# A decoder layer on one core: four instead of six plain tiles in the first feed-forward, scalings on ScalarE, and a split held behind a copy

## The chip, the cores and the metric

The kernel runs on one core of one Trainium2 chip. Its time is the device time in microseconds (us); for the kernel before it is the median of three runs. A profile is one execution, taken by the hardware profiler. The engines are PE (TensorE, matrix multiplication, with PEld for its weight loads), DVE (VectorE), ACT (ScalarE), POOL (GpSimd) and SP, which only issues DMAs.

## What is computed

The reference is one layer of a decoder on 512 tokens of width 1024, all in float32. Cut to what matters here:

```python
x = x + 0.5 * swiglu(rms_norm(x, norm_ffn1_w), ffn1_w_in, ffn1_w_out)   # d_ff = 2816
x = x + hybrid_mixer(rms_norm(x, norm_mix_w), ...)                      # Mamba-2 heads and differential attention
x = x + memory_cross_attention(rms_norm(x, norm_cross_w), ...)
x = x + 0.5 * swiglu(rms_norm(x, norm_ffn2_w), ffn2_w_in, ffn2_w_out)
return rms_norm(x, norm_final_w)

def swiglu(h, w_in, w_out):
    gate, up = split(h @ w_in, 2)
    return (silu(gate) * up) @ w_out
```

## The kernel before

**Products.** A float32 value is split into a rounded high part, which ACT copies out, and the remainder, which DVE subtracts; a product is three matmuls (high by high, high by low, low by high), in `mm3` (L312) and `add_product` (L229). The split of a weight is in `split_into` (L152): ACT writes `wh` (L155), DVE writes `wl` (L156). Weights come by DMA into the buffers `wr`, of which there are six; `wh` and `wl` have three each, so a split waits until the product that used the oldest buffer is over.

**Two ways to make two tiles of the first feed-forward.** The 22 tiles of 128 hidden units (each a gate and an up tile) are made in pairs. By plain products (`proj`, L318) one pair takes 2 tiles x (gate, up) x 8 blocks of the contraction x 3 matmuls of 512 columns. By `quad` (L257) it takes seven block products of the Strassen kind, each of 24 matmuls of 256 columns, in the order "11", S1, S2, "12", S3, S4, "22". The seven weights are four blocks from memory, some of them summed by an accumulating DMA that POOL issues (`raw_w`, L243) or on DVE (`t2` L294, `t4` L297), so a quad has seven splits. Between the products ACT copies accumulators: `b_ps` from `a_ps` (L284 in the first quad of the second feed-forward, L289 elsewhere), `p5` (L292) and `u2` (L299). S3 adds to the bank that `u2` is copied from, so S3 waits for that copy.

**The sums that a quad multiplies.** For each of four pairs of input blocks `block_sums` (L218) scales two blocks by the norm's gain (`fe`, `fo`, L221 and L222, on DVE), forms four half-width sums (L206 to L211), and splits them into `s31h/l` and `s24h/l`. The first feed-forward uses it in `ffn1` (L517), the second in `upd_2` (L1222), right behind the output projection of the cross-attention.

**The first feed-forward** (`ffn1`, L489) goes through `THIRDS`: 6, 8 and 8 hidden tiles. With `NPLAIN = 6` the first third is all plain: two tiles in `ffn_first`, and four in the loop at L510, between which the block sums of the four input pairs are written: two pairs ahead of the first of the four tiles, one ahead of the second, one ahead of the third. The other two thirds are four quads each (`ffn_quads`, L435). A third ends in `out_blocks` (L1271), the product with `w_out`, also by seven block products. It begins with "11" and S1 on the first two pairs of hidden tiles, then takes the last pair; the sums of that last pair are made by DVE and ACT while the first ones are multiplied (`block_tiles`, L456). `next(out)`, at L443 or L526, has its first two weights fetched and split early.

**What sets the order.** The program text sets the order on SP and POOL. On PE, DVE and ACT a scheduler deals the instructions out at compile time, in the order of the text as far as it finds them ready in its own reckoning; each engine then runs its list strictly in that order. `behind(ins)` (L184) forces what is issued inside it after the named instructions of the same engine. `Order` (L57) merges the dense stream of matrix products with side chains: a chain's `yield t` asks to be continued `t` us of reckoned PE time later, and `od.spawn(gen, t)` starts it `t` us later. `beside` (L563) starts chains at the end of each third's hidden tiles: `lambdas` (L596, a small DMA and a few tiny DVE and POOL instructions), `early`, `prepare`.

**Ahead of the second feed-forward** `turn(1, summed=True)` (L1235) transposes the last four blocks of the residual on PE, copies them on ACT (L1242), and squares each on ACT (L551) for the next norm; `row_from` (L553) makes the norm's row out of it, which is needed when the first quad's results are gated.

Of the kernel before, what the change touches and what calls it, by code (L numbers as in the profile page):

```python
# [13 lines left out]
AF = mybir.ActivationFunctionType  # L14
ALU = mybir.AluOpType
# [7 lines left out]
MEM = 256  # L23
EPS = 1e-6

NPLAIN = 6

THIRDS = ((0, 6), (6, 8), (14, 8))
THIRDS2 = ((0, 6), (6, 8), (14, 8))
# [71 lines left out]
def body(tc, a, dbg=None):  # L101
# [116 lines left out]
    def block_sums(k0, gain, blocks, x):  # L218

        fe, fo = s2("fe"), s2("fo")  # L220
        V.tensor_scalar(fe, x[k0], par[:, gain + k0 : gain + k0 + 1], None, ALU.mult)  # L221
        V.tensor_scalar(fo, x[k0 + 1], par[:, gain + k0 + 1 : gain + k0 + 2], None, ALU.mult)  # L222
        return blocks | sums_of(fe[:, :H], fe[:, H:], fo[:, H:], fo[:, :H])

    def of_halves(even, odd):
# [3 lines left out]
    def add_product(ps, w, xs, which, first, ks=None):  # L229

        wh, wl = w
        n = len(xs)
        for f in range(2):
            out = ps[:, f * H : (f + 1) * H]
            for kp in ks or range(n):
                wc = slice((f * n + kp) * P, (f * n + kp + 1) * P)
                xh, xl = xs[kp][which]
                for j, (a_, b_) in enumerate(((wh, xh), (wh, xl), (wl, xh))):
                    od.t += (H + 32) / 2400
                    newest_mm[:] = [nc.tensor.matmul(out, a_[:, wc], b_, start=first and f == 0 and kp == 0 and j == 0, stop=kp == n - 1 and j == 2, skip_group_check=True).ins]  # L240
                yield
# [9 lines left out]
    def split_w(raw):  # L251
        hi = wp.tile([P, D], R32, tag="wh", name=nm("wh"))
        lo = wp.tile([P, D], R32, tag="wl", name=nm("wl"))
        newest[:] = [split_into(hi, lo, raw)[0].ins]
        return hi, lo

    def quad(xs, src, ready, fresh=False):  # L257

        b12, b11, b22, b21 = src[0], src[1], src[2], src[3]
        m1 = raw_w(b11)
        if ready:
            t, t2, m2, m7, m3 = raw_w(ready[0]), raw_w(ready[1]), raw_w(b21), raw_w(b12, b22), raw_w(b22)
            t4 = m2
        else:
            t, m3, m2, m7 = raw_w(b12, b11), raw_w(b22), raw_w(b21), raw_w(b12, b22)  # L270
            t2 = t4 = t
        a_ps = acc("qa")
        e_ps = acc("qe")
        b_ps = acc("qb")
        w1, w5 = split_w(m1), split_w(t)
        second = list(newest)
        if fresh:

            n = len(xs)
            yield from add_product(a_ps, w1, xs, "11", True, range(n - 1))  # L280
            yield from add_product(e_ps, w5, xs, S1, True, range(n - 1))
            yield from add_product(a_ps, w1, xs, "11", False, range(n - 1, n))
            with behind(second):
                S.activation(b_ps, a_ps, AF.Copy)  # L284
            yield from add_product(e_ps, w5, xs, S1, False, range(n - 1, n))
        else:
            yield from add_product(a_ps, w1, xs, "11", True)
            with behind(second):
                S.activation(b_ps, a_ps, AF.Copy)  # L289
            yield from add_product(e_ps, w5, xs, S1, True)  # L290
        p5 = s2("p5")
        S.activation(p5, e_ps, AF.Copy)  # L292
        if not ready:
            V.tensor_tensor(t2, t, m3, ALU.add)  # L294
        yield from add_product(b_ps, split_w(t2), xs, S2, False)
        if not ready:
            V.tensor_tensor(t4, t2, m2, ALU.add)  # L297
        u2 = s2("u2")
        S.activation(u2, b_ps, AF.Copy)  # L299
        V.tensor_tensor(e_ps, e_ps, u2, ALU.subtract)  # L300
        yield from add_product(a_ps, split_w(m2), xs, "12", False)
        w7 = split_w(m7)
        if ready:
            V.tensor_tensor(t4, t2, m2, ALU.add)
        yield from add_product(b_ps, w7, xs, S3, False)
        c22 = s2("c22")
        V.tensor_tensor(c22, p5, b_ps, ALU.subtract)
        yield from add_product(e_ps, split_w(m3), xs, S4, False)
        yield from add_product(b_ps, split_w(t4), xs, "22", False)
        yield (a_ps, b_ps), (e_ps, c22)  # L310

# [177 lines left out]
    def ffn1(h, wa, at_out, each, done):  # L489
        xs = []  # L490
        wq, plain = iter(a["f1q"]), a["f1i"]
        col4, ncol4 = small("col4", 4, bufs=1), small("ncol4", 4, bufs=1)

        for ti, (_, nf) in enumerate(THIRDS):
            g = []
            nq = nf // 2
            made = block_tiles(g, nq, True)
            out = out_blocks(a[f"f1b{ti}"], None, g, col4, ncol4, each if ti == len(THIRDS) - 1 else None, n=nq, by_dma=ti == len(THIRDS) - 1)
            if ti == 0:
                th, f = s4("th"), 0  # L500
                for ps in ffn_first(h, wa):
                    if ps is None:
                        yield
                    else:
                        gated(*ps, st1.row, th, f)
                        f += 1
                made(th)
                V.tensor_scalar(col4, st1.col, 0.5, None, ALU.mult)
                V.tensor_scalar(ncol4, st1.col, -0.5, None, ALU.mult)
                for n in range(NPLAIN - 2):  # L510
                    for i in ((0, 1), (2,), (3,), ())[n]:
                        blocks = of_halves(h[2 * i], h[2 * i + 1])
                        b11 = tuple(s2("h11" + p_, R32, (P, H)) for p_ in "hl")
                        with behind(start):
                            for to, of in zip(b11, blocks["11"]):
                                S.activation(to, of.bitcast(F32), AF.Copy)
                        xs.append(block_sums(2 * i, C_FFN1, blocks | {"11": b11}, xf))  # L517
                    if n == 3:
                        xf.clear()
                    pg, pu = acc("pg"), acc("pu")  # L520
                    yield from proj(pg, load_w(plain[n][0]), h)
                    yield from proj(pu, load_w(plain[n][1]), h)
                    if n % 2 == 0:
                        th = s4("th")
                    if n == NPLAIN - 3:
                        next(out)  # L526
                    gated(pg, pu, st1.row, th, n % 2)
                    if n % 2:
                        made(th)
                h.clear()  # L530
                nq -= NPLAIN // 2
            yield from ffn_quads(xs, wq, st1, nq, made, BY_BLOCK, prime=out)
            at_out(ti)
            if ti == len(THIRDS) - 1:
                xs.clear()
            yield from out
        done()
        banks = [acc, aux, acc, aux]
        yield from turn(1, banks)
        yield from turn(0, banks)  # L540
# [12 lines left out]
    def row_from(st, apart, rows=1.2):  # L553
        both = small("nboth", 4, bufs=2)
        V.tensor_tensor(both, squares[:, :4], squares[:, 4:], ALU.add)
        yield from st.from_sums(both, apart, rows)
# [4 lines left out]
    st_mix, h = Stat(), []  # L561

    def beside(ti):  # L563
        if ti == 0:
            od.spawn(lambdas())
        elif ti == 1:
            od.spawn(early())
        elif ti == 2:
            od.spawn(prepare())
            od.spawn(memory_in(hm), 1.0)  # L570
# [25 lines left out]
    def lambdas():  # L596
        lamv = cp.tile([P, 4, 64], F32, name="lamv")
        nc.sync.dma_start(lamv, a["lam"].partition_broadcast(P))
        yield 8.0
        lamp = small("lamp", 64, bufs=2)  # L600
        lsum = small("lsum", 2, bufs=1)
        for j in range(2):
            V.tensor_tensor(lamp, lamv[:, 2 * j, :], lamv[:, 2 * j + 1, :], ALU.mult)
            V.reduce_sum(lsum[:, j : j + 1], lamp, axis=AX.X)
        yield 4.0
        lexp = small("lexp", 2, bufs=1)
        G.tensor_tensor(lexp, euler[:, 0:1].to_broadcast([P, 2]), lsum, ALU.pow)
        yield 4.0
        V.tensor_tensor(nlam, lexp[:, 1:2], lexp[:, 0:1], ALU.subtract)
        V.tensor_scalar(nlam, nlam, -LAMBDA_INIT, None, ALU.add)  # L610
        V.tensor_scalar(wsub, par[:, C_SUBLN : C_SUBLN + 1], 1.0 - LAMBDA_INIT, None, ALU.mult)
        V.tensor_scalar(dskh, par[:, C_DSKIP : C_DSKIP + 8], 0.5, None, ALU.mult)
# [842 lines left out]
            yield from out_blocks(a[f"f2b{c}"], wsum[c], g, col4, ncol4, *((norm, store) if at_end else (None, None)), clean=c == 0)  # L1455

    def turn_last():
        yield from turn(1, summed=True)
        od.spawn(row_from(st_2, 8.0), 3.0)

    od.add(turn_last())
    od.add(ffn2())
# [89 lines left out]
```

## Time and profile before

| | us |
|---|---|
| runs | 1316.0, 1315.11, 1314.69 |
| median of the runs | 1315.11 |
| the profiled execution's own time | 1314.59 |
| its span, from the first to the last instruction | 1312.7 |

The page of the profile gives each engine's busy time and its share of the span. The view of groups gives for each line, operation and tile how often it ran and how long one took. The view of waits says who waited for whom, how long in total and how often. The timeline lists instructions with their start and length in us; in brackets stands how long the engine sat idle ahead of an instruction, and whom it waited for. The view of windows gives each engine's busy time in a stretch. In "qb<-s31h,wh" the tile in front is written and those behind are read.

The matrix products of the first third of the first feed-forward run from 5.61 to 72.17 us, its output product to 100.98, and the second third begins there. The second feed-forward begins at 972.71 us.

### The profile page before, as it was taken

The page shows a single profiled execution, that of the slowest core. Times are in us where ns is not written, and L with a number is a line of the kernel's source. Part 1 is how long each engine was busy: PE and PEld are TensorE (multiplying, and loading weights), DVE is VectorE, ACT ScalarE, POOL GpSimd, SP SyncE. Part 2 cuts the span into 40 slices and gives each one's busy share as a digit, 9 for nine tenths or more (in the row PEclk, how much of TensorE's full clock was granted, in tenths as well). Part 3 has the DMA queues.
Part 4 walks back from the last instruction along what each step waited for, and adds up shares of the span by engine and source line. Part 5 has one row for each costly group of instructions (what it writes and reads, how often), then busy time and mean ns, then how long its engine had stood idle before and what let it go on. Part 6 is the DMA issues. An engine that isn't in the chain of part 4 may idle for free.

```text
span 1312.7 us, 20086 instructions
## 1 busy us (share of the span) xinstructions
PE 1288.3 (98%) x7708; PEld 1123.4 (86%) x7708; DVE 968.9 (74%) x1538; ACT 708.2 (54%) x1208; POOL 127.8 (10%) x157
## 2 busy tenths in 40 slices
PE   9999999999999999999999999999999999999996
PEld 7889988998887778777788877888889999989995
DVE  6987887787776676467867686645668878877886
ACT  7544564565754564346645465434375646555564
POOL 0001010001010011201003022020001000000001
PEclk9999999999999999999999999999999999999998
DMA  9366778876984434753466558683239776666762
GB/s 339 88 168 185 212 184 211 222 199 162 324 291 145 137 64 133 261 166 105 95 189 173 167 141 238 196 222 120 69 99 274 209 231 181 185 193 180 201 192 82
DMA packets 70415, 237.38 MB, mean 181 GB/s; under 512 B 8288, under 2 KB 9792, under 8 KB 69968
## 3 DMA queue, kind: packets, MB, share of 16 engines
q1 hardware_dynamic: 54352, 183.20, 41.7%
q0 software_dynamic: 13168, 45.67, 19.7%
q10 hardware_dynamic: 2800, 7.23, 1.7%
q8 instruction: 60, 0.98, 0.3%
q14 instruction: 35, 0.29, 0.1%
HBM read 233.92 MB, written 50.91 MB: 217 GB/s over the span
## 4 chain that ended last, share of the span: by engine, by line
PE 58%; issue 10%; DVE 4%; ACT 2%; DMA 2%; POOL 1%; POOLq 0%; ACTq 0%; DVEq 0%
PE pm L146 10%; PE qb L240 8%; PE qe L240 5%; PE qa L240 5%; PE pxbc L146 4%; PE ob L1298 3%; PE pcq L146 3%; PE pz L146 3%; PE oe L1298 2%; PE oa L1298 2%; PE pcv L146 2%; PE pq L146 2%; PE pv L146 1%; PE pk L146 1%; DMA wr<-in_f1b 1%
## 5 line engine op out<-in xcount | busy, mean ns | idle before, releaser
L155 ACT ACTIVATE wh<-wr 128x1024 fp32r<-128x1024 f32 (+1 forms) x329 | 334.2, 1019 | 359.3 <-issue 70.6
L156 DVE TENSOR_TENSOR wl<-wr,wh 128x1024 fp32r<-128x1024 f32 (+1 forms) x329 | 384.8, 1173 | 145.3 <-ACT wh L155 140.2
L777 ACT ACTIVATE ec<-ec,mn 128x512 f32<-128x512 f32 (+3 forms) x64 | 35.4, 554 | 33.7 <-DVE mn L776 33.7
L146 PE MATMUL pxbc<-hnh,wh 128*128 128x512 f32 x128 | 52.6, 411 | 0.0
L146 PE MATMUL pxbc<-hnh,wl 128*128 128x512 f32 x128 | 50.3, 393 | 0.0
L146 PE MATMUL pxbc<-hnl,wh 128*128 128x512 f32 x128 | 50.2, 392 | 0.0
L240 PE MATMUL qb<-s31h,wh 128*128 128x256 f32 x152 | 43.2, 284 | 3.2 <-ACT u L299 3.2
L240 PE MATMUL qb<-s24h,wh 128*128 128x256 f32 x152 | 43.1, 284 | 1.3 <-ACT qb L284 1.3
L240 PE MATMUL qb<-s24h,wl 128*128 128x256 f32 x152 | 43.1, 284 | 0.5 <-DVE wl L156 0.5
L240 PE MATMUL qe<-s31h,wl 128*128 128x256 f32 x152 | 43.1, 284 | 0.2 <-DVE wl L156 0.2
L240 PE MATMUL qa<-h11h,wh 128*128 128x256 f32 x152 | 43.1, 283 | 0.0
L240 PE MATMUL qa<-h11h,wl 128*128 128x256 f32 x152 | 43.0, 283 | 0.0
L240 PE MATMUL qa<-hmh,wh 128*128 128x256 f32 x152 | 43.0, 283 | 0.0
L240 PE MATMUL qa<-hml,wh 128*128 128x256 f32 x152 | 43.0, 283 | 0.0
L240 PE MATMUL qe<-s24h,wh 128*128 128x256 f32 x152 | 43.0, 283 | 0.0
L240 PE MATMUL qe<-s24l,wh 128*128 128x256 f32 x152 | 43.0, 283 | 0.0
L240 PE MATMUL qe<-s24h,wl 128*128 128x256 f32 x152 | 43.0, 283 | 0.0
L240 PE MATMUL qb<-hmh,wh 128*128 128x256 f32 x152 | 43.0, 283 | 0.0
L240 PE MATMUL qb<-hml,wh 128*128 128x256 f32 x152 | 43.0, 283 | 0.0
L240 PE MATMUL qb<-hmh,wl 128*128 128x256 f32 x152 | 43.0, 283 | 0.0
L240 PE MATMUL qa<-h11l,wh 128*128 128x256 f32 x152 | 43.0, 283 | 0.0
L240 PE MATMUL qa<-hmh,wl 128*128 128x256 f32 x152 | 43.0, 283 | 0.0
(453 smaller groups left out, 4158.3 us busy)
## 6 DMA issues: line engine op xcount, KB each, us to landing
wr<-in_f2q SPq DMA_DIRECT2D x44, 512.0 KB, 4.5
wr<-in_f1q SPq DMA_DIRECT2D x40, 512.0 KB, 4.3
wr<-in_f1b SPq DMA_DIRECT2D x30, 512.0 KB, 4.3
isum<-in_f2q SPq DMA_DIRECT2D x22, 512.0 KB, 6.2
wr<-isum SPq DMA_DIRECT2D x22, 512.0 KB, 4.6
wsum<-in_f2b SPq DMA_DIRECT2D x20, 512.0 KB, 6.7
wr<-wsum SPq DMA_DIRECT2D x20, 512.0 KB, 4.6
wr<-in_f1q POOLq DMA_DIRECT2D x16, 512.0 KB, 6.5
```

The source lines that it names most:

```text
L146: newest_mm[:] = [nc.tensor.matmul(out, w, x, start=start, stop=stop).ins]
L155: S.activation(hi, src, AF.Copy),
L156: V.tensor_tensor(lo, src, hi.bitcast(F32), ALU.subtract),
L240: newest_mm[:] = [nc.tensor.matmul(out, a_[:, wc], b_, start=first and f == 0 and kp == 0 and j == 0, stop=kp == n - 1 and j == 2, skip_gr ...
L777: S.activation(ec[:, :n], ec[:, :n], AF.Exp, bias=mn, scale=-1.0, accum_out=sm[c][:, i : i + 1])
L1298: newest_mm[:] = [nc.tensor.matmul(ps, a_[:, ts], b_[:, ws], start=first and k == 0 and j == 0, stop=k == n - 1 and j == 2, skip_group_che ...
```

## The change

`NPLAIN` goes from 6 to 4, so the first third is two tiles of `ffn_first`, two plain tiles in the loop and one quad in place of the last two plain tiles; all four block sums are written ahead of the second of the two remaining tiles. `next(out)` moves with it, to the last quad. `block_sums` scales on ACT instead of DVE, in both feed-forwards. In every quad the split of `m3`, the sixth weight, is held behind the copy `u2` on ACT. The chain `lambdas` starts 30 us after the hidden tiles of the second third instead of right after those of the first. The squares ahead of the second feed-forward leave `turn` and become a chain of their own, `row_of_last`, which starts 4 us later, does one square every 2 us, each behind the newest weight split on ACT, and then makes the row.

```diff
-NPLAIN = 6
+NPLAIN = 4
...
     def block_sums(k0, gain, blocks, x):
 
         fe, fo = s2("fe"), s2("fo")
-        V.tensor_scalar(fe, x[k0], par[:, gain + k0 : gain + k0 + 1], None, ALU.mult)
-        V.tensor_scalar(fo, x[k0 + 1], par[:, gain + k0 + 1 : gain + k0 + 2], None, ALU.mult)
+        S.activation(fe, x[k0], AF.Copy, scale=par[:, gain + k0 : gain + k0 + 1])
+        S.activation(fo, x[k0 + 1], AF.Copy, scale=par[:, gain + k0 + 1 : gain + k0 + 2])
...
         u2 = s2("u2")
-        S.activation(u2, b_ps, AF.Copy)
+        copy = S.activation(u2, b_ps, AF.Copy)
...
-        yield from add_product(e_ps, split_w(m3), xs, S4, False)
+        with behind([copy.ins]):
+            w3 = split_w(m3)
+        yield from add_product(e_ps, w3, xs, S4, False)
...
                 for n in range(NPLAIN - 2):
-                    for i in ((0, 1), (2,), (3,), ())[n]:
+                    for i in ((0, 1), (2, 3))[n]:
...
-                    if n == 3:
-                        xf.clear()
...
-                    if n == NPLAIN - 3:
-                        next(out)
                     gated(pg, pu, st1.row, th, n % 2)
...
                 h.clear()
+                xf.clear()
...
-        if ti == 0:
-            od.spawn(lambdas())
-        elif ti == 1:
+        if ti == 1:
+            od.spawn(lambdas(), 30.0)
             od.spawn(early())
...
     def turn_last():
-        yield from turn(1, summed=True)
-        od.spawn(row_from(st_2, 8.0), 3.0)
+        yield from turn(1)
+        od.spawn(row_of_last(), 4.0)
+
+    def row_of_last():
+        for k in range(4, KT):
+            with behind(list(newest)):
+                squared(k, x[k])
+            yield 2.0
+        yield from row_from(st_2, 3.0)
```

## The prediction

> **What bounds the kernel now.** I read the shares of the engines first, then what PE waits for, then the timeline at those waits.
>
> ```profile
> PE 1288.3 (98%) x7708; PEld 1123.4 (86%) x7708; DVE 968.9 (74%) x1538; ACT 708.2 (54%) x1208; POOL 127.8 (10%) x157
> ```
>
> PE is busy 98% of the span. A change can shorten the work that PE does, or close one of its gaps. The view of PE's waits lists the gaps:
>
> ```profile
> PE qb L240 <- ACT u L299: 3.2, 2, 1.6
> ...
> PE qb L240 <- ACT qb L284: 1.3, 1, 1.3
> ...
> PE oe L1298 <- DVE s31l L156: 0.7, 1, 0.7
> ...
> PE qb L240 <- DVE wl L156: 0.5, 1, 0.5
> ...
> PE qe L240 <- DVE wl L156: 0.2, 1, 0.2
> ```
>
> Total, times and longest, in us. Two lines are what this change aims at: two waits for the copy `u2` (3.2 in all) and one for the copy `qb` (1.3). The others are small, so everything else that could be gained is PE's own work.
>
> **The change part by part.**
>
> *A quad in place of two plain tiles.* From the chain of work, one gate or up tile by plain products, and one block product of a quad:
>
> ```profile
> 569.35 5.44 PE pk L146 x24
> ...
> 1067.14 2.88 PE qe L240 x24
> ```
>
> 24 matmuls of 512 columns take 5.44 us (227 ns each), 24 of 256 columns 2.88 us (120 ns each, a little over half). The pair leaves with 4 x 5.44 = 21.76 and the quad comes with 7 x 2.88 = 20.16: **-1.60 us**.
>
> [...]
>
> *The split behind the copy.* The timeline of ACT in a quad that goes well, in one that doesn't, and PE in the latter:
>
> ```profile
> 231.44 1.06 ACT L155 ACTIVATE wh<-wr 128x1024 fp32r<-128x1024 f32 x1 [0.90 <-PE qb L240]
> 232.40 0.58 ACT L299 ACTIVATE u<-qb 128x512 f32<-128x512 f32 x1
> ...
> 251.65 1.06 ACT L155 ACTIVATE wh<-wr 128x1024 fp32r<-128x1024 f32 x1 [1.34 <-issue]
> 252.61 0.61 ACT L155 ACTIVATE s31h<-s 128x512 fp32r<-128x512 f32 x1
> 254.54 1.06 ACT L155 ACTIVATE wh<-wr 128x1024 fp32r<-128x1024 f32 x1 [1.31 <-PE qa L240]
> 255.50 0.58 ACT L299 ACTIVATE u<-qb 128x512 f32<-128x512 f32 x1
> ```
>
> ```profile
> 256.13 0.39 PE L240 MATMUL qb<-s31h,wh 128*128 128x256 f32 x1 [1.58 <-ACT u L299]
> ```
>
> S2 is over at about 251.6 in the second quad, and `u2` could be copied then. But two weight splits stand ahead of it in ACT's list: the sixth, at 251.65, and the seventh, which waits until PE has finished "12" (`qa`). The copy runs at 255.50 and PE is 1.58 late. With the sixth split behind the copy, the seventh, which follows the sixth in the text, comes behind it too. The second occurrence is alike, so both waits go: **-3.15** (3.2 by the row, two waits of just under 1.6). The delayed sixth split costs nothing: the copy puts it off by 0.58, it takes ACT 1.06 and DVE some 1.2, and S4, which uses it, starts two products (5.76) after S2's end. Next late is nothing on PE: "12" runs on meanwhile.
>
> *The squares leave the start of the second feed-forward.* ACT and PE there:
>
> ```profile
> 976.96 0.61 ACT L551 ACTIVATE junk<-x 128x512 f32<-128x512 f32 x1
> ...
> 979.41 0.57 ACT L284 ACTIVATE qb<-qa 128x512 f32<-128x512 f32 x1
> ...
> 987.99 0.60 ACT L407 ACTIVATE row<-nrow 128x512 f32<-128x512 f32 x1 [0.91 <-PE nrow L146]
> ```
>
> ```profile
> 977.71 0.28 PE L240 MATMUL qa<-h11h,wl 128*128 128x256 f32 x1
> ...
> 980.03 0.38 PE L240 MATMUL qb<-s24h,wh 128*128 128x256 f32 x1 [1.33 <-ACT qb L284]
> ```
>
> `qa` is complete at 977.99, but ACT does four squares from 976.96 on, until it copies at 979.41. Without them the copy runs at about 978.05 and ends at 978.65, when PE needs it: **-1.33**, or -1.2 if a square still gets in. The row is then made later: 4.0 + 4 x 2.0 + 3.0 + 1.2 = 16.2 us behind the quad's start at 972.7, some 989, so the copy `row` moves from 987.99 to about 990. It is needed when the quad ends, 20.16 after 972.7, at 992.9. The cover is 3 us; if it were gone, the gating would be late and hold PSUM banks. The four squares then stand among weight splits on an ACT that is 54% busy; I cost them at nothing.
>
> *The scalings go to ACT.* Prices from the timeline: two scalings in a row on DVE, and ACT's operation with a scale column on a tile of the same size:
>
> ```profile
> 37.25 0.48 DVE L221 TENSOR_SCALAR fe<-xf,par 128x512 f32<-128x512 f32 x1
> 37.65 0.48 DVE L222 TENSOR_SCALAR fo<-xf,par 128x512 f32<-128x512 f32 x1
> ```
>
> ```profile
> 4.31 0.72 ACT L159 ACTIVATE hmh<-xf,par 128x512 fp32r<-128x512 f32 x1 [1.99 <-DMA xf<-in_xT]
> ```
>
> Eight per feed-forward: DVE is relieved of 8 x 0.40 = 3.2 us, ACT gets 8 x 0.72 = 5.8. In the second feed-forward this lies beside the output projection, and only the last pair is close to PE:
>
> ```profile
> 976.30 0.69 DVE L156 TENSOR_TENSOR s31l<-s,s31h 128x512 fp32r<-128x512 f32 x1
> ```
>
> It ends at 976.99, and S1 wants it 0.12 behind the `qa` row above, at 977.83. Two scalings of 0.72 take the place of two of 0.40 in its chain, 0.64 longer, which the 0.84 of slack covers; one of the two blocks is ready a tile earlier. I cost it at nothing; uncovered it is 0.6.
>
> *The first third.* Here the engine that matters is DVE. The windows from the end of `ffn_first` to the third plain tile, and from there to `out_blocks` (columns: PE, PEld, DVE, ACT, POOL busy; clock; DMA share; GB/s):
>
> ```profile
> 28.15:50.41 22.26, 22.26 (x99) 18.39 (x98) 20.12 (x43) 13.49 (x22) 1.09 (x1) 1.00 0.48 132
> 50.41:72.17 21.76, 21.76 (x97) 18.02 (x96) 18.07 (x32) 9.68 (x15) 1.84 (x2) 1.00 0.32 80
> ```
>
> DVE is busy 20.12 + 18.07 = 38.19 of 22.26 + 21.76 = 44.02. The fourth pair's sums end like this on DVE:
>
> ```profile
> 56.82 0.69 DVE L156 TENSOR_TENSOR s31l<-s,s31h 128x512 fp32r<-128x512 f32 x1
> 57.42 1.22 DVE L156 TENSOR_TENSOR wl<-wr,wh 128x1024 fp32r<-128x1024 f32 x1
> 58.56 0.69 DVE L156 TENSOR_TENSOR s24l<-s,s24h 128x512 fp32r<-128x512 f32 x1
> ```
>
> The change takes from DVE 3.2 of scalings, four plain splits at 1.14 (57.42 to 58.56), three gating operations of 0.6 (taken as long as the `s31l` from 56.82 to 57.42) and, estimated, 1.0 for the six tiny ones of `lambdas`; it adds seven splits (8.0), two weight sums of the same size (2.3) and three accumulator operations at 0.6 (1.8): 38.2 - 3.2 - 4.6 - 1.8 - 1.0 + 12.1 = 39.7 in 42.4 us. It fits by 2.7. If DVE idles as much as now (44.02 - 38.19 = 5.8), PE is late by 39.7 + 5.8 - 42.4 = **3.1** at most. For the start: the quad begins at 50.41, S1 wants the fourth `s31l` after "11" and nine matmuls, 50.41 + 2.88 + 1.08 = 54.4, S2 the fourth `s24l` at 57.3. Even left where they stand, and only relieved of 3.2, these end at 54.3 and 56.05; the text also puts them one tile earlier. So I take **+0.8** out of 0 to 3.1. ACT goes from 13.49 to at most 19.3 in the first window's 22.26, which fits.
>
> The weights are no wait: the quad's five loads and two accumulating DMAs are asked for behind four loads instead of eight, and land in 9.1 and 6.5 us by these rows, one after the other 15.6, ahead of 50.41 if asked for by 34:
>
> ```profile
> wr<-in_f1q POOLq DMA_DIRECT2D x16, 512.0 KB, 6.5
> ...
> wr<-in_f1i SPq DMA_DIRECT2D x8, 512.0 KB, 9.1
> ```
>
> On SP the two early loads of `out_blocks` now stand behind the quad's five, and are wanted only when the quad ends; `lambdas`' load and POOL's one power move into the second third's output product, between loads issued ahead of need: nothing.
>
> *The end of the first third.* After a quad, gating, the last pair's sums and their splits must be done while PE works on the earlier pairs. Three such ends, PE's first matmul behind the quad and the moment of `s31l`, in the second feed-forward's first third, and the first one's second and third thirds:
>
> ```profile
> 1035.52 0.40 PE L1298 MATMUL oa<-wh,g11h 128*128 128x512 f32 x1
> ...
> 1042.34 0.39 PE L1298 MATMUL oe<-wh,s31h 128*128 128x512 f32 x1
> ```
>
> ```profile
> 1041.41 0.69 DVE L156 TENSOR_TENSOR s31l<-s,s31h 128x512 fp32r<-128x512 f32 x1
> ...
> 193.05 0.69 DVE L156 TENSOR_TENSOR s31l<-s,s31h 128x512 fp32r<-128x512 f32 x1
> ...
> 315.17 0.69 DVE L156 TENSOR_TENSOR s31l<-s,s31h 128x512 fp32r<-128x512 f32 x1
> ```
>
> ```profile
> 183.09 0.40 PE L1298 MATMUL oa<-wh,g11h 128*128 128x512 f32 x1
> ...
> 307.02 0.40 PE L1298 MATMUL oa<-wh,g11h 128*128 128x512 f32 x1
> ```
>
> With three pairs the cover is 1042.34 - 1035.52 = 6.82. `s31l` was done after 6.58, 10.65 and 8.84, the last two with weight sums in between on DVE, as here, though half of ours are half as wide. The cost is 0 to 10.65 - 6.82 = 3.83; between the nearest two (0 and 2.0) I take **+1.0**. A plain end has no such wait.
>
> Sum: -1.60 - 3.15 - 1.33 + 0.8 + 1.0 = **-4.28**. Against the profiled execution's own 1314.59 (span 1312.7) that is 1310.31; the median of the runs stands 0.52 higher, 1315.11, and gives **1310.8 us**.
>
> **The rivals.**
>
> *No new wait at all*: -6.08, or -7.5 if the 0.5, 0.2 and 0.7 in the waits go as well in the new order: 1307.6 to 1309.0. For it: DVE's slack, and the 6.58 against 6.82. Against: 96% of DVE asked for in a strict order.
>
> *The first third pays it back*: DVE late by the full 3.1 and the end by 3.83: -6.08 + 6.93 = +0.85, 1316.0.
>
> *The edge does not free the copy*: the scheduler deals the seventh split, which has no edge of its own, ahead of `u2` again. The seventh was what held it at 254.54. Then 3.15 stays: -1.1, 1314.0. Against: it comes behind the sixth in the text.
>
> *Slower: DVE waits for ACT at each scaling.* The scalings are now at the head of each pair's chain and in ACT's strict list, behind copies and splits that themselves wait. The same handover in DVE's waits:
>
> ```profile
> DVE wl L156 <- ACT wh L155: 140.2, 145, 4.7
> ```
>
> That is 0.97 each. If each of the eight scalings of the first third costs DVE that much, 7.8 come on top of 3.1: -6.08 + 10.9 = +4.8, **1319.9**. It decides from 8.7 of new waits on, which turns the sign past 0.2%. Against: `xf` has long landed, so ACT can scale ahead of need; it is free for 22.26 - 13.49 = 8.8 us of the first window. [...]
>
> **How the numbers follow.** Forecast 0.50; no new wait 0.12; paid back 0.14; edge fails 0.07; slower 0.17. 0.2% is 2.6 us, about what a measurement of this kernel can tell from no change. So faster 0.62, same 0.21, slower 0.17. The range from 1307.5 to 1318 takes in all but the slower rival and a few lucky cases.
>
> **What would show it.** Right: the quad's seven products of 2.88 us from about 50.4; no row of PE waiting for `u` L299, nor for `qb` L284; DVE at 9 tenths or more from 28 to 70 us; a wait of `oe` or `oa` for `g11l` or `s31l` near 77 us of 0 to 2. Wrong: waits of PE for `wl`, `s31l`, `s24l` in the first quad that add up to more than 3, or a later part, whose order this change should leave alone, dealt differently.

## The result, and the profile after

| | kernel before | kernel after |
|---|---|---|
| median of four runs each | 1315.55 us | 1329.3 us |
| lowest and highest | 1314.69, 1317.23 | 1324.54, 1332.88 |
| profiled execution | 1314.59, span 1312.7 | 1332.88, span 1330.8 |

The ratio of the times is 1.0099, with an interval of 1.0076 to 1.0123: the change makes the kernel about 1% slower, where 0.3% faster was forecast. The profiled execution is the longest of the four.

The view of PE's waits of the kernel after (total, times, longest, in us) answers to the five lines shown of before:

```profile
PE qe L240 <- ACT gate L430: 5.3, 1, 5.3
PE ob L1296 <- ACT wh L155: 5.2, 2, 4.2
...
PE ob L1296 <- DVE wl L156: 1.1, 1, 1.1
PE oa L1296 <- ACT g11h L155: 1.0, 1, 1.0
...
PE qb L240 <- ACT qb L284: 0.8, 1, 0.8
PE oa L1296 <- DVE g11l L156: 0.8, 1, 0.8
```

What the change aimed at came about: no row for `u` L299 is left, and the copy `qb` L284 costs 0.8 instead of 1.3. But there are two new waits of over 4 us, and some of about 1.

The view of windows, cut at PE's first matmul of six stages of the first feed-forward, shows where the time went. The stages are the last two tiles of the first third (plain before, a quad now), the first third's output product, the second third's quads and output product, and the third third's. Columns are PE, PEld, DVE, ACT, POOL busy, then the granted clock, DMA share and GB/s. First the kernel after, then the rows of before that the prediction does not show:

```profile
52.77:80.68 27.91, 22.64 (x170) 22.34 (x169) 21.07 (x31) 13.06 (x18) 0.86 (x1) 0.88 0.31 83
80.68:111.11 30.43, 29.33 (x130) 23.69 (x128) 26.70 (x38) 15.73 (x22) 2.57 (x3) 1.00 0.69 186
111.11:193.45 82.34, 81.15 (x674) 80.74 (x673) 68.50 (x82) 45.39 (x56) 7.76 (x9) 1.00 0.73 193
193.45:235.51 42.06, 40.30 (x171) 32.60 (x169) 32.35 (x41) 19.87 (x23) 3.15 (x4) 0.96 0.75 205
235.51:318.17 82.66, 81.63 (x674) 80.97 (x673) 67.81 (x84) 45.90 (x63) 8.00 (x10) 1.00 0.77 197
318.17:366.70 48.53, 43.21 (x174) 33.22 (x173) 36.35 (x50) 27.16 (x45) 4.24 (x5) 0.93 0.82 235
```

```profile
72.17:100.98 28.81, 28.81 (x128) 23.84 (x127) 24.68 (x35) 14.44 (x20) 2.61 (x3) 1.00 0.74 203
...
183.09:222.50 39.41, 38.71 (x170) 31.38 (x169) 33.02 (x39) 20.10 (x23) 3.45 (x4) 1.00 0.81 220
222.50:307.02 84.52, 81.37 (x675) 80.91 (x674) 66.36 (x81) 46.59 (x63) 6.91 (x8) 1.00 0.80 206
307.02:347.75 40.73, 40.21 (x174) 31.36 (x173) 34.92 (x49) 27.24 (x45) 4.30 (x5) 1.00 0.79 234
```

Read pairwise: the quad that took the place of two plain tiles takes 27.91, not less than the pair's 21.76 (+6.15). The first third's output product has 1.6 more, the second third's 2.65. The third third's quads, where the two waits for `u2` were, have 1.86 less. The third third's output product has 7.8 more. Three of the rows of after have a granted clock below 1.00, and the rows of before have none. These five differences add up to 16.4 of the 18.1 by which the spans differ. Another 2.4 stands at the very start of this execution, where PE's matmuls of 512 columns begin 0.43 us apart up to 11.1 us, while in the kernel before they begin 0.23 apart from 7.05 on, and the loop's plain tiles begin at 30.97 instead of 28.61; the later versions of the changed kernel, with the same start, have them between 28.5 and 29.3, so this is no effect of the change. The rest of the kernel is about 0.7 shorter.

**The first quad.** The timeline of the kernel after, PE and then DVE:

```profile
61.31 0.55 PE L240 MATMUL qe<-s31h,wh 128*128 128x256 f32 x1 [5.27 <-ACT gate L430]
...
56.41 1.22 DVE L297 TENSOR_TENSOR wr<-wr,wr 128x1024 f32<-128x1024 f32 x1
...
58.14 1.22 DVE L156 TENSOR_TENSOR wl<-wr,wh 128x1024 fp32r<-128x1024 f32 x1
59.28 0.69 DVE L156 TENSOR_TENSOR gl<-th,gh 128x512 fp32r<-128x512 f32 x1
...
60.48 0.68 DVE L435 TENSOR_TENSOR th<-pu,gate 128x512 f32<-128x512 f32 x1
```

The pool `acc` has four PSUM banks. The plain tiles' `pg` and `pu` have them all, so the quad's `qa` gets the bank of the first `pg`, and `qe`, which S1 writes, that of the first `pu`. That `pu` is read for the last time by the product at L435, 60.48 to 61.16, and S1 starts at 61.31. All that it reads was there some 12 us earlier: `pu` was complete at 42.05, and its gate was begun on DVE at 47.26. But it writes `th`, of which there is one buffer, and that buffer is still read by `gl`, the split of the two tiles before; and `gl` stands behind the last pairs' sums and the quad's own weight sums in DVE's list. The kernel before has the same chain, and nobody waits, since `gl` runs at 50.76 and the product is over at 52.64:

```profile
50.76 0.69 DVE L156 TENSOR_TENSOR gl<-th,gh 128x512 fp32r<-128x512 f32 x1
...
51.96 0.68 DVE L433 TENSOR_TENSOR th<-pu,gate 128x512 f32<-128x512 f32 x1
```

Its next `pu` takes that bank at 55.85, with 3.2 to spare. Now `gl` comes 8.5 later (59.28), and the 3.2 become the 5.3 that PE waits. Counted from the stage's first matmul, `gl` comes 6.2 later (6.51 instead of 0.35), and the bank is wanted 2.2 sooner, since "11" is shorter than the `pg` that stood there. (The view names the ACT gating at L430 as the releaser, that of the second tile. It ended last, at 61.23, but it works on `gate`, which is in no PSUM bank; the run with a second buffer below shows that the chain is the one described.)

**The clock behind it.** The windows of after ahead of S1, during S1, and during S2:

```profile
55.90:61.31 5.41, 0.14 (x1) 0.03 (x1) 5.31 (x8) 2.68 (x5) 0.00 (x0) 0.80 0.14 34
61.31:66.30 4.99, 4.99 (x25) 4.99 (x26) 1.74 (x4) 0.73 (x2) 0.00 (x0) 0.54 0.04 16
66.30:69.20 2.90, 2.90 (x27) 2.90 (x26) 1.66 (x3) 2.06 (x3) 0.00 (x0) 1.00 0.00 0
```

S1 takes 4.99 instead of 2.88 at a granted clock of 0.54. The wait of 5.27 costs 2.1 more than itself.

**The last output product.** The timelines of before and of after around the second of the two weight sums for S2 (the `wr<-wr,wr` on DVE). It frees a `wr` buffer, into which SP loads (L1279, L1277) the second part of the weights for S3; POOL accumulates on it (L1318, L1316); ACT splits it.

```profile
315.77 1.22 DVE L1328 TENSOR_TENSOR wr<-wr,wr 128x1024 f32<-128x1024 f32 x1
...
317.02 0.33 SPq L1279 DMA_DIRECT2D wr<-in_f1b  x1
...
322.37 0.86 POOL L1318 DMA_DIRECT2D wr<-in_f1b  x1 [2.07 <-DMA wr<-in_f1b]
...
331.91 1.06 ACT L155 ACTIVATE wh<-wr 128x1024 fp32r<-128x1024 f32 x1 [2.29 <-DMA wr<-in_f1b]
```

```profile
331.77 1.22 DVE L1326 TENSOR_TENSOR wr<-wr,wr 128x1024 f32<-128x1024 f32 x1
...
333.02 0.33 SPq L1277 DMA_DIRECT2D wr<-in_f1b  x1
...
340.11 0.86 POOL L1316 DMA_DIRECT2D wr<-in_f1b  x1 [7.56 <-DVE hm L160]
...
348.77 1.06 ACT L155 ACTIVATE wh<-wr 128x1024 fp32r<-128x1024 f32 x1 [8.49 <-DMA wr<-in_f1b]
...
349.88 0.79 PE L1296 MATMUL ob<-wh,s31h 128*128 128x512 f32 x1 [4.22 <-ACT wh L155]
```

The output product begins at 307.02 and 318.17. Counted from there, the sum came at 8.75 and comes at 13.6 now; SP's load starts as it ends, 10.0 and 14.85; POOL's accumulation comes at 15.35 and 21.9, and ACT's split at 24.9 and 30.6. PE waits 4.22, and runs the next 6.2 us at a granted clock of 0.50.

### The profile page after: what moved, and what is told of

It is laid out like the page before. It is cut to its first block, busy times and chain, and to the rows that moved or that the text cites. A ratio compares the mean times of both kernels' runs of the same rounds, so it can differ in the third digit from the quotient of the medians.

```text
span 1330.8 us, 20257 instructions
## 1 busy us (share of the span) xinstructions
PE 1295.8 (97%) x7780; PEld 1131.9 (85%) x7780; DVE 972.0 (73%) x1528; ACT 721.6 (54%) x1229; POOL 130.4 (10%) x159
## 4 chain that ended last, share of the span: by engine, by line
PE 72%; issue 14%; DVE 6%; DMA 3%; ACT 3%; POOL 2%; POOLq 0%; SPq 0%; ACTq 0%; DVEq 0%
PE qb L240 12%; PE pm L146 10%; PE qe L240 8%; PE qa L240 8%; PE pxbc L146 4%; PE ob L1296 4%; PE oa L1296 4%; PE pcq L146 3%; PE pz L146 3%; PE oe L1296 3%; DVE wl L156 2%; PE pa L146 2%; PE pcv L146 2%; PE pq L146 2%; DMA wr<-in_f1q 1%
## 5 line engine op out<-in xcount | busy, mean ns | idle before, releaser
L240 PE MATMUL qe<-s31h,wh 128*128 128x256 f32 x160 | 46.3, 290 | 5.3 <-ACT gate L430 5.3
L240 PE MATMUL qe<-s31h,wl 128*128 128x256 f32 x160 | 46.3, 289 | 0.7 <-DVE wl L156 0.7
L240 PE MATMUL qe<-s31l,wh 128*128 128x256 f32 x160 | 46.2, 289 | 0.0
L240 PE MATMUL qb<-s31l,wh 128*128 128x256 f32 x160 | 45.3, 283 | 0.0
L240 PE MATMUL qb<-s31h,wl 128*128 128x256 f32 x160 | 45.3, 283 | 0.0
```

## The experiments

Each kernel is timed against the kernel before on the same chip. The kernel before came to 1315.22, 1316.46 and 1316.64 in three sets of runs made for this, so a difference between medians of different sets is good to about 1 us. My theory after the result was that three things had gone wrong separately: the bank behind `th` in the first quad, DVE's list in the last output product, and the clock behind each. The rivals were that one edit (the four plain tiles, or the scalings) costs the time by its work, or that the split's new place does not gain.

**The split behind the copy alone** (the kernel before with the edit of `quad`)

```diff
-        S.activation(u2, b_ps, AF.Copy)
+        copy = S.activation(u2, b_ps, AF.Copy)
...
+        with behind([copy.ins]):
+            w3 = split_w(m3)
```

> The kernel before with the edge alone: the sixth split behind the copy u2. Theory (the change's parts gain as priced, the loss comes from the first third and what its waits set off): both waits of PE for the copy, 3.15 us, go, so about 3.2 less than the kernel before, 1312.3, and no row of PE waiting for u. Rival (the edge deals the whole ACT list anew and costs elsewhere): no gain, or 1316 and more.

Measured: 1321.7 us (1315.27 to 1324.75), ratio 1.004 [1.0023, 1.0057]. The expectation failed, and its rival (a list dealt anew that costs elsewhere) came true, though in DVE's list. The rows for `u` L299 are gone, but this edit alone brings the late weights of the last output product. Its timeline there, where the output product begins at 305.78:

```profile
320.72 1.22 DVE L1330 TENSOR_TENSOR wr<-wr,wr 128x1024 f32<-128x1024 f32 x1
...
321.96 0.33 SPq L1281 DMA_DIRECT2D wr<-in_f1b  x1
...
329.81 0.86 POOL L1320 DMA_DIRECT2D wr<-in_f1b  x1 [8.05 <-DMA wr<-in_f1b]
...
338.84 1.06 ACT L155 ACTIVATE wh<-wr 128x1024 fp32r<-128x1024 f32 x1 [9.61 <-DMA wr<-in_f1b]
...
339.95 0.80 PE L1300 MATMUL ob<-wh,s31h 128*128 128x512 f32 x1 [5.33 <-ACT wh L155]
```

The edit stands in another function than the weight sum. The scheduler reckons the whole program through, and with the quads reckoned differently it deals the second sum out behind two updates of `x` and some splits, at 14.9 instead of 8.75.

**The squares in a chain alone** (the kernel before with the edits of `turn_last` and `row_of_last`)

> The kernel before with only the four squares moved out of the turn into a chain of their own. Theory: the wait of 1.33 for the copy qb shrinks to the 0.8 that the changed kernel shows, so 0.5 to 1.3 us less, within the noise of one run: 1314.2 to 1315.0. Rival (the row comes too late and the gating of the first quad holds PSUM): PE waits of over 1 us behind 990 us, 1316 to 1318.

Measured: 1314.93 us, ratio 0.9998 [0.9989, 1.0008]; the wait for `qb` L284 is 0.8 instead of 1.3. So the edit gains 0.5 of a wait where I gave it 1.33, too little for the times to show, and does no harm. ACT's timeline in the changed kernel shows what is late next, a weight split that itself waits until PE is done with `qa`:

```profile
996.38 1.06 ACT L155 ACTIVATE wh<-wr 128x1024 fp32r<-128x1024 f32 x1 [0.26 <-PE qa L240]
997.34 0.58 ACT L284 ACTIVATE qb<-qa 128x512 f32<-128x512 f32 x1
```

**Four plain tiles alone** (the kernel before with `NPLAIN = 4` and the loop that goes with it; the scalings on DVE, `lambdas` in the first third)

> The kernel before with four instead of six plain tiles alone (block sums of all four pairs ahead of the second of the two tiles, scalings still on DVE, lambdas, squares and the split as before). Theory (the quad in the first third brings the wait for its bank and what follows it): -1.6 for the products, +5 to +9 for the wait since eight scalings of 0.4 stand in DVE's list again, +2 for the clock, 0 to 3 at the thirds' ends: 1321 to 1328. Rival (the scalings on ACT are the cause): without them the quad fits, 1314 to 1316.

Measured: 1325.88 us, ratio 1.0084 [1.006, 1.0108]. PE's longest wait in it:

```profile
PE qe L240 <- DVE lamp L600: 7.0, 1, 7.0
```

The wait for the bank is there without the other edits, and is longer (7.0 against 5.3), so the other edits taken together shorten it. It isn't all that this kernel loses: the second third's quads, which were not edited, take 86.4 against 82.1, with a wait of 1.88 for a weight's split and a granted clock of 0.54 in the 6.3 us behind it. (The releaser named, `lamp`, is the DVE instruction that came last; it writes no bank.)

**The changed kernel with a buffer of its own for the plain tiles' product**

```diff
                     if n % 2 == 0:
-                        th = s4("th")
+                        th = s4("gate")
```

The buffer of that name is free until the first quad's gating.

> The changed kernel, with the result of the two plain tiles of the loop written to the idle buffer named gate instead of the single buffer th. Theory: the 5.27 us that S1 of the first quad waits are a chain of buffers (S1's bank is free once the plain tile's th is written, th once the last split of the tiles before has read it), and the 2.26 that S1 then takes longer are the clock at half after the idle stretch. With the second buffer both go: 1329.3 - 7.5 = 1321.8, and PE's S1 follows 11 within 1 us. Rival (DVE is simply full, the buffer only the last in line): PE waits as long for s31l or wl of the quad, 1328 and more.

Measured: 1321.79 us, ratio 1.005 [1.0031, 1.0069], 7.5 below the changed kernel. The wait of 5.27 and the half clock behind it are gone (the matmuls of S2 and S1 there begin 0.12 us apart); this shows the chain from `gl` through `th` to the bank: `gl` is as late as ever (57.55), but the product of the first `pu` runs at 46.56. The scheduler now also deals S2 to PE ahead of S1, so next late is S2:

```profile
PE qb L240 <- ACT qb L289: 2.5, 2, 1.8
```

The 1.8 is in the first quad: ACT's copy stands behind the fourth `s24h`, which waits for DVE's last pair of sums. This is the lateness of DVE that the prediction had named.

**The changed kernel with PE kept busy in the wait.** 23 more matmuls of ones go into the bank that `out_blocks` clears, in the first third alone; nothing reads them.

```diff
-        if clean:
+        for _ in range(24 if early and sums[3] is not None and n == 3 and not by_dma else 1 if clean else 0):
             nc.tensor.matmul(b_ps[1], ones_r, ...)
```

> The changed kernel with 23 more matmuls of ones into the cleared bank, dealt to PE where it waits 5.3 us in the first quad. They compute nothing that is used. Theory (the half clock behind that wait comes from PE having been idle): the first quad's S1 starts as late as before but takes 2.9 to 3.1 us instead of 5.14, the granted clock there is 1.0, and the time is 1329.3 less 2.3, about 1327. Rival (the clock is lowered by something else, the load of the stretch ahead): S1 still takes about 5 and the time stays at 1329.

Measured: 1324.95 us (1321.03 to 1327.19, against 1324.54 to 1332.88 of the changed kernel), ratio to before 1.0062 [1.0043, 1.0081]. The windows of the filled wait and of S1 behind it:

```profile
53.96:59.63 5.67, 5.65 (x27) 4.35 (x25) 5.57 (x9) 2.81 (x5) 0.00 (x0) 1.00 0.13 33
59.63:62.60 2.97, 2.97 (x25) 2.97 (x26) 1.74 (x4) 0.74 (x2) 0.00 (x0) 1.00 0.07 26
```

S1 starts as late behind "11" as in the changed kernel and takes 2.97 at a granted clock of 1.00, against 4.99 at 0.54. So here the half clock came with PE's idling, and not from the work around it. The gain of 4.4 is more than the 2.3 expected, but the runs of both kernels spread by 6 to 8; the profile also has a granted clock of 1.00 from 50 to 340 us, the end of the second third in it, where the changed kernel has 0.73 from 199.76 to 206.00.

**Both weight sums ahead of the updates** (the kernel before with the split behind the copy)

```diff
+        by_t2 = sums[2]
+        if here:
+            w2 = {part: t2(part) for part in parts}
+            by_t2 = lambda part: w2[part]
         for t in range(2):
             update(t + 2, 1, e_ps[t], 1, False)
-        yield from product(b_ps, sums[2], S2)
+        yield from product(b_ps, by_t2, S2)
```

> The kernel before with the split behind the copy alone, and in the output product of a third both weight sums for S2 taken ahead of the two updates of x. Theory (the split's new place re-deals DVE's list, so that the second weight sum of the last third falls behind the updates, and the load that needs its buffer goes out 5 us late): the second sum comes about 9 us after the end of the last third's quads instead of 14.9, ScalarE's wait for the last accumulated weights falls from 9.6 to about 2.5, PE's 5.3 at the output's last products is gone and so is the half clock behind it; 1321.7 falls by 5.3 + 3 to about 1313. Rival (the late weights come from the queue of accumulating transfers or from SP's loads, not from the sum's place): the wait of 5.3 stays and the time is within 1 us of 1321.7.

Measured: 1314.54 us, ratio 0.9988 [0.9979, 0.9997], some 7 below the run with the split alone. PE's wait of 5.33 and the half clock behind it are gone; the mean granted clock of the profiled execution is 0.997, against 0.995 with the split alone. The second sum comes at 11.2 (the output product begins at 303.79), earlier than 14.9 but not as early as the 9 that I expected. PE now waits for something smaller, the first part's split, which DVE does behind both sums and the updates:

```profile
315.03 1.22 DVE L1330 TENSOR_TENSOR wr<-wr,wr 128x1024 f32<-128x1024 f32 x1
...
319.76 0.50 PE L1300 MATMUL ob<-wl,s24h 128*128 128x512 f32 x1 [2.10 <-DVE wl L156]
```

Nothing but the place of the sums and their loads in the text was changed, so it is that place that made the 5.3. The last output product takes 51.22 in the run with the split alone, 43.31 here and 40.73 in the kernel before, so in this stage the new place takes back most of what the split had cost and gains nothing beyond it. The new place without the split was not run.

**The same with the squares in a chain**

> As the one before, with the squares of the second turn in a chain of their own as well. Theory: the gains add, 3.15 at the copies of the sixth product, less about 0.9 of new waits for the seventh, and 0.5 at the squares: 2 to 3 below the kernel before, 1312 to 1313. Rival (a wait removed in this list comes back somewhere else each time): 1315 to 1322.

Measured: 1314.9 us, ratio 0.9985 [0.9972, 0.9997]: less than expected. Its profile has the same wait as the run ahead of it, 2.14 against 2.10, but here the clock fell behind it, to a mean of 0.61 against 1.00. The window that follows the wait, here and then in the run ahead of it:

```profile
320.00:323.50 3.50, 3.50 (x10) 2.77 (x11) 2.91 (x4) 0.88 (x1) 1.64 (x4) 0.61 0.76 140
```

```profile
319.80:323.30 3.50, 3.50 (x16) 2.89 (x17) 3.50 (x5) 1.14 (x3) 1.54 (x4) 1.00 0.74 147
```

Ten matmuls against sixteen in 3.5 us.

**The changed kernel with the buffer and the sums**

> The changed kernel with the plain tiles' product of gate and up in a buffer of its own and the two weight sums ahead of the updates. Theory: 1321.8 of the run with the buffer alone, less 3.2 of PE's wait in the last third and about 1.7 of the half clock behind it: about 1317, so the change without its two accidents is still not below the kernel before (1315.2), since the end of the second third keeps a wait of 1.8 and a half clock behind it. Rival (the changed kernel's gain of 3.15 + 0.5 + 1.6 stands once both accidents are gone): 1311 to 1312.

Measured: 1315.59 us, ratio 0.9997 [0.9987, 1.0007]. Without its two accidents the change comes to no measurable difference. This is 1.4 below what I expected, and still 4 above what the rival claimed.

**Six plain tiles, with the first sum's split ahead of the second sum**

```diff
+            first_t2 = weights(t2, parts[0])
+            w2 = {part: t2(part) for part in parts[1:]}
...
+        yield from product(b_ps, by_t2, S2, ready=first_t2)
```

> The kernel before with the split behind the copy, the squares in a chain, both weight sums ahead of the updates, and the first sum's split ahead of the second sum. Theory (what is left of the loss in the last third's output is the order of DVE's list alone): PE's wait of 2.1 at the second part of S2 falls to 0.7 or less, no half clock stands behind it, and the time comes to 1312, 3 below the kernel before. Rival (the wait comes from a load): 1314 to 1315.

Measured: 1314.09 us (1311.22 to 1316.79) against 1316.64 of the kernel before in the same set of runs, ratio 0.9968 [0.9956, 0.998]. This beats both kernels. The wait of 2.1 is now 0.8, and the clock is at 1.00 throughout that stage. The medians differ by 2.6, the ratio makes it 4.2, and the spans of the two profiled executions differ by 1.4; the two gains come to 3.6. In the profiles 0.7 of this is lost at the start of the execution and 1.9 in the last output product, against some 0.5 gained elsewhere. That product now begins 2.3 earlier, and ACT waits for a load at a place where the kernel before has no such wait; that the early begin is the reason is my reading, and no run tests it:

```profile
310.66 1.06 ACT L155 ACTIVATE wh<-wr 128x1024 fp32r<-128x1024 f32 x1 [2.72 <-DMA wr<-in_f1b]
```

Its output product takes 42.65 (304.70 to 347.35) against 40.73.

**Four plain tiles with the same repairs**, and two variants of it: `lambdas` in the first third again, and the scalings on DVE again (each of these by undoing its lines of the change)

> The changed kernel with a buffer of its own for the plain tiles' product, and the sums and the split ahead of the updates as in the run with six plain tiles. It differs from that run by the four plain tiles, the scalings on ScalarE and the lambdas' later place. Theory (those three cost more in the first third than the 1.6 that a quad saves, 1.85 at S2's bank and about 2 in the output product, and 1.3 at the end of the second third): about 1315, 3 above the other run. Rival (the 1.6 stands): 1310.5.

> The run before it with the lambdas computed in the first third again, as in the kernel before. Theory (the second third's end is late because the lambdas now run in it): PE's waits of 0.5 and 0.8 for g11 at that end go, the first third's wait at S2's bank grows by up to 1; the time is within 1 of 1315. Rival (that end is late from the first third's shift or the weights): both waits stay.

> The run with four plain tiles and both repairs, with the scalings on VectorE again. Theory (VectorE is the late engine of the first third; 8 scalings of 0.48 stand ahead of the first quad): PE's wait at S2's bank grows from 1.85 to 3 to 4, and the time to 1317 or 1318. Rival (VectorE has room there): the wait and the time stay as without it, about 1315.

Measured: 1315.88 us, ratio 0.9995 [0.9983, 1.0007], for the first; 0.9993 [0.9981, 1.0006] with `lambdas` early; 1319.76 us, 1.0021 [1.0011, 1.0031], with the scalings on DVE. So four plain tiles are 1.8 us by the medians and 0.27% by the ratios above six with the same repairs, and scalings on DVE cost 3.9 more. `lambdas` moves nothing that can be measured. Of the second third's end, the profile of the first run has neither wait for `g11`, the one with `lambdas` early has 0.8 for `g11l` again: the theory that `lambdas` makes that end late is wrong, and what does is still open.

With the scalings on DVE the first quad has waits of 1.33 for `qb` L289, 1.07 for `s24h` and 0.69 for a weight: 3.1 against 1.85, as expected of a late DVE. But this is not the whole 3.9. By the profiles the stage of the first quad is 1.1 longer than in the first run (25.06 against 23.97), or 2.5 longer than with `lambdas` early (22.59, at a granted clock of 1.00); another 2.1 lies in the last output product (43.37 against 41.26), which has no scalings in it. What the quad itself brings is seen where the granted clock is 1.00: the windows of six plain tiles, then those of four with `lambdas` early.

```profile
51.12:72.88 21.76, 21.76 (x97) 18.03 (x96) 18.07 (x32) 9.67 (x15) 1.92 (x2) 1.00 0.33 82
72.88:101.70 28.82, 28.82 (x129) 23.85 (x128) 24.73 (x35) 14.33 (x20) 2.62 (x3) 1.00 0.74 197
...
223.25:304.70 81.45, 81.37 (x674) 80.92 (x673) 66.01 (x81) 45.89 (x63) 6.90 (x8) 1.00 0.76 198
```

```profile
50.90:73.49 22.59, 20.74 (x171) 20.37 (x169) 21.23 (x35) 12.42 (x17) 1.71 (x2) 1.00 0.37 88
73.49:103.89 30.40, 29.32 (x130) 23.70 (x128) 26.69 (x38) 15.71 (x22) 2.61 (x3) 1.00 0.72 199
```

PE's work falls by 1.02 (21.76 to 20.74), but the stage is 0.83 longer, since PE now idles 1.85 in it. The output product behind it is 1.58 longer, 1.08 of it a wait for `wl`.

## Why the prediction was wrong

**The quad, -1.60.** Right in kind: PE works 1.02 less in that stage; of the 0.58 that is missing, 0.40 is the matmul of ones that clears a bank, which I had not counted and which now runs in this stage. With the two repairs the stage and its output product together are still 2.41 longer than with six plain tiles.

**The split behind the copy, -3.15.** Right where it was looked for: the third third's quads go from 84.52 to 81.45 (-3.07) in the best version, and no wait for `u2` is left. Of the rivals, "the edge does not free the copy" is out.

**The squares, -1.33.** Mis-sized: 0.5. I took the copy to be next on ACT once the squares are gone; a weight split of 1.06 is.

**The first third, +0.8 out of 0 to 3.1.** This step failed. I added up DVE's work and asked when the fourth pair's sums would be ready. That lies in the range: with the bank's chain cut, what is left is one wait of 1.85 for just these sums. What I left out is that three gating operations in that sum also release PSUM banks. The first of them stands behind a split that waits its turn in DVE's list, and S1 needs the bank at once. I counted them as 0.6 us each, and they cost 5.27 and a granted clock of 0.54 behind it. The rows of before would have shown it: `gl` at 50.76, `th` over at 52.64, and a bank that is wanted at 55.85 and so has 3.2 to spare, in a list ahead of which the change puts sums and weight sums.

**The rival "DVE waits for ACT at each scaling"** had the right sign and the wrong mechanism. Against DVE, scalings on ACT gain 3.9 in the last run, 1.1 to 2.5 of it where they are made.

**The end of the first third, +1.0.** No wait for `s31l` came there. The output product was 1.6 longer all the same, mostly by a wait for `wl` in its fifth product.

**"A later part, whose order this change should leave alone."** This failed, and was the dearest: 7.8 in the last output product, and 2.65 in the second, of which I know only the rows: waits of 0.98 and 0.79 for `g11h` and `g11l` and a granted clock of 0.73 from 199.76 to 206.00. Why these two come late there stays open. I treated an edit in `quad` as local, although the front of this document says that the scheduler deals instructions out as it finds them ready in its own reckoning. The last output product needs its second weight sum early, since a load, an accumulating transfer and a split hang on it one after the other; the lists of before happened to have it there. In the run with the split alone the sum's lateness of 6.2 reached SP's load in full and POOL's accumulation as 8.7: the load took 7.85 until POOL could go on, not 5.35. Why that load took longer was not tried.

**The clock.** My sum had no term for it. In the kernel after, both waits of over 4 us were followed by a lower one: behind the 5.27, S1 of the first quad lost 2.1 at a granted clock of 0.54, and behind the 4.22 the last output product lost some 3, an estimate from 6.2 us at 0.50, on top of the wait itself.

The two accidents account for the time: 7.5 by the run with the buffer (1329.3 to 1321.79) and 6.2 more by the one with the sums ahead of the updates as well (to 1315.59), 13.7 of the 13.75 between the two kernels. These medians are of different sets; the ratios say the same, 1.0099, 1.005 and 0.9997. Without both, the change is even with the kernel before. By the profile it gains 2.8 in the third third's quads and 0.9 in the second's, and loses 2.4 in the first third on the four plain tiles, 1.5 in the second third's output product and 0.6 in the last one.

## What to carry to other kernels

An edit under a compile-time scheduler is not local: before its gain is counted, the engine lists of both kernels are to be compared through to the end, above all where a short instruction starts a chain of transfers. When a stage is replaced, it is not enough to add up each engine's work: for each buffer and each PSUM bank that the new stage takes over, find the instruction that frees it, and what that instruction stands behind. A wait of PE is to be priced with the lower clock that can follow it (here the granted clock was 0.54 behind a wait of 5.27, and behind waits of about 1.8 it was 0.66 in one run and 1.00 in another), and a fixed place for the few instructions on which transfers hang is worth more than a shaved wait elsewhere.

## What the runs showed of the hardware

The views of windows give the granted clock behind some of PE's waits, as a mean over a stretch. The stretch at the end of the second third has the waits in it.

| run, place | PE idle ahead, us | stretch, us | granted clock |
|---|---|---|---|
| split alone, last output product | 5.33 | 339.90 to 346.00 | 0.50 |
| changed kernel, first quad | 5.27 | 61.31 to 66.30 | 0.54 |
| changed kernel, last output product | 4.22 | 349.80 to 356.00 | 0.50 |
| split, sums and squares, last output product | 2.14 | 320.00 to 323.50 | 0.61 |
| split and sums, last output product | 2.10 | 319.80 to 323.30 | 1.00 |
| four plain tiles alone, second third | 1.88 | 114.70 to 121.00 | 0.54 |
| four plain tiles with the repairs, first quad | 1.8 | 58.00 to 62.00 | 0.66 |
| the same with early `lambdas`, first quad | 1.85 in all | 58.00 to 62.00 | 1.00 |
| changed kernel, end of the second third | 0.98 and 0.79 | 199.76 to 206.00 | 0.73 |
| PE kept busy, first quad | 0.02 | 59.63 to 62.60 | 1.00 |

Behind the three waits of over 4 us in this table the clock was at 0.50 to 0.54; with PE kept busy in the place of one of them it was at 1.00. Two more such waits show in the matmuls behind them: with four plain tiles alone, those of S1 begin 0.21 us apart up to 63.6, behind a wait of 6.97, and 0.12 apart from 64.0 on; with PE kept busy in the first quad, four in the last output product take 0.63 to 0.79 each behind a wait of 4.80, against 0.39 to 0.40 in the split alone from 347 on. Nearly equal waits of about 2 us were not always followed by the same clock: 2.14 by 0.61 and 2.10 by 1.00, 1.8 by 0.66 and 1.85 by 1.00. What decides between them is not shown.
